# Where six-part modulation vectors are computed: parts moved from matmuls beside the linear attention to VectorE beside the MLPs

## The chip, the cores and the metric

The kernel runs on one core of a Trainium2 chip. Its time is the device time of one execution in microseconds (us), lower is better. The engines are named as in the profile: PE (TensorE's matmuls, PEld its weight loads), DVE (VectorE), ACT (ScalarE), POOL (GpSimd) and SP (the queue that issues most DMAs).

## The reference

Two layers process 512 latent tokens and 256 context tokens of width 1024 in float32. Each layer scales and shifts its normalised input with vectors that depend on a conditioning vector ("adaLN"). There are six parts of 1024 columns for each layer, and they are needed for the latent stream (from `c`) and, in layer 0 and for the first two parts of layer 1, for the context stream (from `c_ctx`):

```python
mod_l = jnp.split((jax.nn.silu(c) @ ada_w[layer] + ada_b[layer])[:, None, :], 6, axis=-1)
mod_c = jnp.split(jax.nn.silu(c_ctx) @ ada_w[layer] + ada_b[layer], 6, axis=-1)
ul = modulate(lat, g[0], mod_l[0], mod_l[1])            # mixer input
lat = lat + mod_l[2] * rmsnorm(yl @ w_out[layer], g[1])
lat = lat + mod_l[5] * rmsnorm(sq_relu_mlp(modulate(lat, g[2], mod_l[3], mod_l[4]), mlp_w1[layer], mlp_w2[layer]), g[3])
if ctx_out:                                             # layer 0 only: the same for cx with mod_c
    ...
```

So part 5 of layer 0 is first needed behind the second product of layer 0's MLP, parts 0 and 1 of layer 1 right behind that, parts 2 to 4 behind layer 1's mixer, and part 5 of layer 1 at the very end. Layer 0 mixes with gated linear attention beside grouped-query attention, layer 1 with an mLSTM beside retention. One part is a vector times a 1024 x 1024 matrix, 4 MB of weights.

## The kernel before

**Order of the work.** The program runs startup (parts 0 and 1 of layer 0, first projections), the linear attention stage ("GLA"), softmax attention, the output projection, the MLP of layer 0 over 768 tokens, the mixer of layer 1, its output projection, and the MLP of layer 1 over 512 tokens. The source order is written out by hand in strings (`PLAN`, line 133): each letter is one step of a generator. In "gla", `G` is a quarter of one of four head pairs of the linear attention, `q` a tile of the query projection, `a` one step of modulation, `l` a deferred piece of query preparation. In "mlp", `h` is a hidden tile (first product), `P` a piece of the second product, `s` one step of modulation from the side generator. Both strings of "mlp" are used for blocks 0 to 5 of eight; block 6 has a fixed string with nine `s`, and the last product calls the side generator at four of its token tiles ("side", line 139). The framework then orders the instructions of each engine by that source order and by its own cost estimates, so an engine's final order is near the source order, not equal to it.

**Matmuls.** A float32 product is made as three products of rounded halves (`mm3`, lines 488 to 490). The high half is a cast on ACT (`split`, L197), the low half a subtraction on DVE (L198). Weights pass through `raw`, a ring of three 128 x 1024 tiles that weights and modulation loads share; split weights go into rings of five. In the MLP the second product is made with seven instead of eight block products, for which POOL subtracts weight blocks (L638), DVE subtracts activations (L675) and adds up results (L744, first ones copied on ACT, L742).

**Modulation in the GLA stage** (`ada_steps`, L245): two parts at a time, eight steps; each step loads two 512 KB tiles (issue L257) and makes four column-tiled matmuls (L260, 32 of 128 columns each, both streams at once, each recorded as two instructions). `ada_finish` (L267) then fills two tiles on POOL (L271, L272), loads bias and gain, adds on DVE (L280) and stores. Three pairs of parts are made so: layer 0 parts 2 and 3, layer 0 parts 4 and 5, layer 1 parts 0 and 1.

**Modulation in layer 0's MLP** (`ada_part`, L293): layer 1 parts 2 to 5, latent stream only. A part has two column halves; each is summed over eight row blocks on DVE (first L310, then seven times L312, all 128 x 512), four loads of 512 KB (issue L303) to a half. A `yield` stands behind each issue, so one `s` treats the tile loaded by the `s` before and issues the next load. Then two matmuls with a matrix of ones (L315) sum over the partitions into a PSUM tile of tag "B", which the hidden tiles use too, and `ada_rows` (L319) fills two tiles on POOL (L324, L325), loads bias and gain (L329, L331), adds and scales on DVE (L332, L333) and stores (L335). The accumulators are a ring of two (`sp` in pool `p5`).

Of the kernel before, what the change touches and what calls it, by code (L numbers as in the profile page):

```python
# [8 lines left out]
F32 = mybir.dt.float32  # L9
# [3 lines left out]
ALU = mybir.AluOpType  # L13
# [109 lines left out]
def const_offsets():  # L123
# [8 lines left out]

PLAN = {
    "start": "tttttt",
    "gla": "GaGaGaqGaalGaaGalaqaaaGaGGlGlaaaqGaaaGaGlGlaqGGaaa",
    "att": "QQSSSSQSSSfSVSfSSSVSfSSSVfQSSSVSSVSSSVfQfVSSVVSfVSVQSSVSSVfVSVSSVSVSSVSVSVMSVSMVVSSVSSSVVSVMVVVVVVVM",
    "pre": 7,
    "l1": "tPPPtPPDtPPPPPPPLPzzPPPLzzFgUFLFwgULBgFwgwwwYUwwMBMMMBURBRRwR",
    "side": [1, 2, 3, 4],
    "mlp": ["sPhPPshPPhsPPhsP", "PhPPhPPhPPhP"],  # L140
    "ahead": (3, 3),
}

# [1 line left out]
class Kern:  # L145
# [144 lines left out]
                nc.sync.dma_start(out=cut(md[j]), in_=bt[r, :])  # L290
            self.mod[layer, part] = (md, 0)

    def ada_part(self, layer, part, pool):  # L293

        nc = self.nc
        W = self.a["ada_w"][layer]
        c0 = part * 1024
        md = self.T(self.dram, [1, 1024])
        acc = [self.T(pool, [128, 512], F32, tag="sp", bufs=2) for _ in range(2)]
        for x in range(2):  # L300
            for kk in range(4):
                raw = self.T(self.w1, [128, 1024], F32, tag="raw", bufs=3)
                nc.sync.dma_start(out=raw.rearrange("p (k n) -> p k n", k=2),  # L303
                                  in_=W[kk * 256:(kk + 1) * 256, c0 + x * 512:c0 + (x + 1) * 512].rearrange("(k p) n -> p k n", p=128))
                yield
                for k in range(2):
                    w = raw[:, k * 512:(k + 1) * 512]
                    c = self.sT[:, 2 * kk + k, 0:1]
                    if kk == 0 and k == 0:
                        nc.vector.tensor_scalar(out=acc[x], in0=w, scalar1=c, scalar2=None, op0=ALU.mult)  # L310
                    else:
                        nc.vector.scalar_tensor_tensor(out=acc[x], in0=w, scalar=c, in1=acc[x], op0=ALU.mult, op1=ALU.add)  # L312
        ps = self.pb()
        for x in range(2):
            nc.tensor.matmul(ps[32 * x:32 * x + 32, :], self.ones, acc[x], start=True, stop=True)  # L315
        self.ada_rows(layer, part, ps, [(0, 0), (512, 0)], md)
        self.mod[layer, part] = (md, 0)

    def ada_rows(self, layer, part, ps, rows, md):  # L319
# [837 lines left out]
    def layer0(self):  # L1157
        nc, a = self.nc, self.a
        uT = self.new_uT(self.r1, TOK)
        acc = self.startup(uT)  # L1160
# [3 lines left out]
        with self.pool("mx") as mx:  # L1164
# [11 lines left out]
            with self.pool("ga") as ga:  # L1176
                self.C0 = self.load_consts(ga, _L0_CONST)
                lr = self.T(ga, [128, 6, 32])

                def ev0(t, ps):  # L1180
                    nc.scalar.copy(ak[:, t * 128:(t + 1) * 128], ps[:, 0:128])
                    nc.scalar.copy(av[:, t * 128:(t + 1) * 128], ps[:, 128:256])
                    nc.vector.tensor_copy(lr[:, t], ps[:, 256:288])
                self.proj_tok(W, [(2080, 256), (1536, 32)], uT, range(NT), ev0, True)
                gv = self.big(self.r2)
                tok4 = lambda ap, t: ap[:, :, t * 128:(t + 1) * 128]
                self.proj_tok(W, [(512, 512)], uT, range(NT),
                              lambda t, ps: nc.scalar.copy(tok4(gv, t), ps.rearrange("p (r n) -> p r n", r=4)), True)
                kst = self.att_keys(ak, gb, tabs[1])

                late = []

                def later(n=1):
                    for x in late:
                        for _ in range(n):
                            next(x, None)

                def ev2(t, ps):
                    late.insert(0, self.att_query(t, ps, gb, tabs[0], qs_d[t * 128:(t + 1) * 128, :]))
                    later()  # L1200
                qsteps = self.proj_steps(W, [(1568, 512)], uT, range(NT), ev2)
                ada = (x for layer, parts in ((0, (2, 3)), (0, (4, 5)), (1, (0, 1))) for x in self.ada_steps(layer, parts, self.po()))
                gla = self.gla(ga, [gqk[:, p] for p in range(4)], [gv[:, p] for p in range(4)], lr,
                               lambda p: nc.sync.dma_start(out=on_d[p * 128:(p + 1) * 128, :], in_=gqk[:, p]))
                ops = {"G": lambda: next(gla), "q": lambda: next(qsteps), "a": lambda: next(ada, None), "l": later}
                for c in PLAN["gla"].replace(" ", ""):
                    ops[c]()
                later(2)
                for _ in ada:
                    pass  # L1210
# [42 lines left out]
        with self.pool("xw", bufs=3) as xw, self.pool("h0") as h0:  # L1253
            with self.pool("p3") as p3:
                self.out_proj(0, ws, lambda i, k: (yT[i] if k < 4 else yA[i])[:, k % 4], self.x_in,
                              lambda t: self.xs1[t * 128:(t + 1) * 128, :], uT2, p3, xw, range(NT), 0)
            with self.pool("p5") as p5, self.pool("ya") as yap:
                ytile = lambda dt=F32: self.T(yap, [128, 1024], dt, tag="y", bufs=6)
                ya, mods, cur, rvw = [], {}, [], []
                W1 = a["cd_w_in"][0]  # L1260
                self.rv_d = self.T(self.dram, [TOK, 512])

                def acc(t):
                    if t == len(ya):
                        ya.append(ytile())
                    return ya[t]

                def rv_weights(k):
                    if k == 1:
                        big = self.T(self.r1, [128, 3072], F32R, tag="big", bufs=4)  # L1270
                        cur[2:] = [big[:, i * 1024:(i + 1) * 1024] for i in range(3)]
                    into = {0: None, 1: cur[2:4], 2: [ytile(F32R), ytile(F32R)] if k == 2 else None, 3: [cur[4], ytile(F32R)] if k == 3 else None}[k]
                    rvw.extend(self.w_unit(W1, [(2048, 512)], k, into))

                def done(t, m, y, ss):
                    stream = "ctx" if t < 2 else "lat"
                    if not mods:
                        self.next_u = self.new_uT(self.r2, TOK)
                        mods["ctx"] = [self.bcast(xw, l, part, "ctx", "xh", 3) for l, part in ((0, 5), (1, 1), (1, 0))]
                        big = self.T(self.r1, [128, 3072], F32, tag="big", bufs=4)  # L1280
                        mods["lat"] = [self.bcast(None, l, part, "lat", None, tile=big[:, i * 1024:(i + 1) * 1024])
                                       for i, (l, part) in enumerate(((0, 5), (1, 1), (1, 0)))]
                    gg, gs, sh = mods[stream]
                    if m == 0:
                        cur[0:2] = [self.T(xw, [128, 1024], F32, tag=tag, bufs=3) for tag in ("xl", "xl" if t < 2 else "xh")]
                    xt, u = cur[0:2]
                    nc.vector.tensor_tensor(out=u[:, m * 512:(m + 1) * 512], in0=y, in1=gg[:, m * 512:(m + 1) * 512], op=ALU.mult)
                    if m == 0:
                        nc.sync.dma_start(out=xt, in_=self.xs1[t * 128:(t + 1) * 128, :])
                        return  # L1290
                    for k in {0: (0,), 1: (1,), 3: (2,), 4: (3,)}.get(t, ()):
                        rv_weights(k)
                    self.post_halves(ss, xt, u, self.xs2[t * 128:(t + 1) * 128, :])
                    self.prep(xt, gs, sh, u, self.next_u, t * 128)

                self.ones = self.T(h0, [128, 32])
                nc.vector.memset(self.ones, 1.0)

                def side():

                    for part in range(2, 6):
                        yield from self.ada_part(1, part, p5)
                ada = side()
                full = [(0, 512), (512, 768)]
                self.mlp(0, uT2, TOK, (self.r1, self.r1), h0, acc, xw, (full, full), done, ada)
                for _ in ada:
                    pass
                for _ in self.spill_tok(2048, self.next_u, range(NT), self.rv_d, False, True, rvw, p5):
                    pass
# [375 lines left out]
    def layer1(self):  # L1685
# [101 lines left out]
        with self.pool("xw1", bufs=3) as xw, self.pool("h1") as h1, self.pool("p7") as p7:  # L1787
# [9 lines left out]
            def done(i, m, y, ss):  # L1797
# [7 lines left out]
                (nc.gpsimd if i == 3 and m == 0 else nc.vector).tensor_tensor(out=yg[:, m * 512:(m + 1) * 512], in0=y, in1=mods[0][:, m * 512:(m + 1) * 512], op=ALU.mult)  # L1805
                if m:
                    self.post_halves(ss, xt, yg, self.out[0, i * 128:(i + 1) * 128, :])
            self.mlp(1, uT3, 512, (self.r2, self.r2), h1, acc, xw, ([(0, 256), (256, 512)], [(0, 512)]), done)

    def body(self):  # L1810
        tc, nc = self.tc, self.nc
# [39 lines left out]
```

## Time and profile before

| what | value |
|---|---|
| median of three runs | 1749.84 us (1747.56 to 1750.02) |
| the profiled execution | 1746.07 us |
| its span, first to last instruction | 1744.4 us |
| mean granted TensorE clock | 0.981 of 2.4 GHz |
| busy share of the span | PE 95%, PEld 75%, DVE 65%, ACT 45%, POOL 15% |
| moved by DMA | 193.74 MB read, 25.30 MB written, mean 127 GB/s |

A wait is written "engine line <- releaser line". Times in windows are from the span's start. Stages by their instructions: startup to about 120 us, GLA 120 to 280, attention and output projection to about 505, layer 0's MLP to about 985, layer 1's mixer and output projection to about 1420, layer 1's MLP to the end. A matmul's duration includes its passage through the pipeline, so matmuls in a row overlap; the busy time counts such overlap once.

### The profile page before, as it was taken

What the parts mean: (1) busy time and instruction counts of PE and PEld (TensorE: products, weight loads), DVE (VectorE), ACT (ScalarE), POOL (GpSimd) and SP (SyncE); (2) the same over time, 40 slices, a digit from 0 to 9 for tenths busy, and PEclk for the clock granted to TensorE, in tenths of its full rate; (3) what the DMA queues carried; (4) which work ended last, traced back from release to release, by engine and by line L of the source; (5) the groups of instructions that cost most, each with busy time, mean ns of one, the idle gap of its engine ahead of it and who ended that gap; (6) DMA issues with size and microseconds to landing.
All of it is one profiled execution on the core that took longest, in us unless ns stands there. A gap on an engine that the chain in (4) does not pass through costs nothing.

```text
span 1744.4 us, 25127 instructions
## 1 busy us (share of the span) xinstructions
PE 1660.3 (95%) x9795; PEld 1316.5 (75%) x9795; DVE 1131.3 (65%) x1678; ACT 791.5 (45%) x1392; POOL 264.3 (15%) x216
## 2 busy tenths in 40 slices
PE   7998999999999999999999999978998999999998
PEld 5775555755778888888888878757887788888876
DVE  5435456465678558657668693466786676777876
ACT  5335435464345434334333454635552355445443
POOL 0000020100002211121120000164011112223210
PEclk9999999999999999999999999988996999999999
DMA  9415666231654224224123552234545533333322
GB/s 289 129 52 178 202 205 223 72 91 37 205 169 128 90 61 155 74 83 157 62 90 118 176 192 64 84 104 130 161 132 164 181 98 108 110 108 99 107 86 84
DMA packets 174746, 220.67 MB, mean 127 GB/s; under 512 B 17450, under 2 KB 112742, under 8 KB 174628
## 3 DMA queue, kind: packets, MB, share of 16 engines
q1 hardware_dynamic: 169444, 201.24, 36.7%
q0 software_dynamic: 5184, 17.83, 3.0%
q8 instruction: 77, 1.26, 0.3%
q14 instruction: 41, 0.34, 0.1%
HBM read 193.74 MB, written 25.30 MB: 126 GB/s over the span
## 4 chain that ended last, share of the span: by engine, by line
PE 77%; DVE 9%; DMA 6%; ACT 4%; issue 3%; SPq 1%; POOL 0%; DVEq 0%; ACTq 0%; POOLq 0%
PE x L488 21%; PE x L489 21%; PE x L490 21%; DMA x<-in_ada_w_dram 2%; PE x L1116 2%; PE x L260 2%; DVE x L198 2%; PE x L1107 1%; PE x L1093 1%; DMA x<-x 1%; ACT x L197 1%; PE x L1542 1%; PE x L957 1%; PE x L435 1%; PE x L1681 1%
## 5 line engine op out<-in xcount | busy, mean ns | idle before, releaser
L488 PE MATMUL x<-x,x 128*128 128x512 f32 (+2 forms) x2042 | 763.3, 375 | 12.1 <-ACT x L197 3.4
L489 PE MATMUL x<-x,x 128*128 128x512 f32 (+2 forms) x2050 | 762.8, 373 | 7.1 <-DVE x L198 7.1
L490 PE MATMUL x<-x,x 128*128 128x512 f32 (+2 forms) x2050 | 761.1, 372 | 0.1
L198 DVE TENSOR_TENSOR x<-x,x 128x1024 fp32r<-128x1024 f32 (+4 forms) x373 | 395.5, 1079 | 216.5 <-ACT x L197 211.4
L197 ACT CAST x<-x 128x1024 fp32r<-128x1024 f32 (+4 forms) x373 | 332.7, 911 | 388.4 <-PE x L489 181.3
L488 PEld LDWEIGHTS x<-x,x 128*128 128x128 f32 x2042 | 387.4, 190 | 91.1 <-ACT x L197 9.0
L489 PEld LDWEIGHTS x<-x,x 128*128 128x128 f32 x2050 | 389.1, 190 | 75.7 <-DVE x L198 11.7
L490 PEld LDWEIGHTS x<-x,x 128*128 128x128 f32 x2050 | 388.9, 190 | 70.6 <-issue 6.3
L638 POOL TENSOR_TENSOR x<-x,x 128x1024 f32<-128x1024 f32 x56 | 145.5, 2599 | 546.3 <-DMA x<-in_mlp_w_dram 250.2
L744 DVE TENSOR_TENSOR x<-x,x 128x512 f32<-128x512 f32 x225 | 143.9, 680 | 12.3 <-PE x L490 11.2
L689 ACT ACTIVATE x<-x 128x512 f32<-128x512 f32 (+4 forms) x96 | 44.3, 477 | 91.2 <-PE x L490 91.2
L312 DVE SCALAR_TENSOR_TENSOR x<-x,x,x 128x512 f32<-128x512 f32 x56 | 53.1, 948 | 20.8 <-DMA x<-in_ada_w_dram 19.9
L260 PE MATMUL x<-x,x 128*32 128x512 f32 x192 | 45.6, 604 | 7.5 <-DMA x<-in_ada_w_dram 7.4
L690 ACT ACTIVATE x<-x 128x512 f32<-128x512 f32 (+4 forms) x96 | 48.0, 516 | 2.1
L1095 DVE TENSOR_REDUCE x<-x 128x1 f32<-128x768 f32 (+1 forms) x48 | 36.6, 775 | 18.9 <-PE x L1093 18.7
L1116 PE MATMUL x<-x,x 128*64 128x512 f32 x112 | 44.2, 618 | 1.0 <-ACT x L1110 0.7
L1096 ACT ACTIVATE x<-x,x 128x768 f32<-128x768 f32 (+1 forms) x48 | 36.3, 757 | 12.5 <-DVE x L1095 12.3
L1107 PEld LDWEIGHTS x<-x,x 128*128 128x128 f32 x224 | 24.5, 141 | 22.9 <-issue 21.1
L675 DVE TENSOR_TENSOR x<-x 128x768 f32<-128x768 f32 (+1 forms) x28 | 38.4, 1371 | 0.0
L1093 PE MATMUL x<-x,x 128*128 128x256 f32 (+1 forms) x160 | 36.7, 347 | 1.3 <-ACT x L1096 1.3
L799 DVE TENSOR_REDUCE x<-x 128x8 f32<-128x512 f32 (+1 forms) x19 | 14.3, 753 | 35.5 <-ACT x L797 35.4
L797 ACT ACTIVATE x<-x 128x512 f32<-128x512 f32 (+1 forms) x19 | 12.8, 673 | 47.6 <-PE x L957 25.8
(316 smaller groups left out, 1517.8 us busy)
## 6 DMA issues: line engine op xcount, KB each, us to landing
x<-in_mlp_w_dram SPq DMA_DIRECT2D x128, 512.0 KB
x<-in_ada_w_dram SPq DMA_DIRECT2D x96, 512.0 KB
x<-x SPq DMA_DIRECT2D x42, 512.0 KB
x<-x SPq DMA_DIRECT2D x50, 256.0 KB
x<-in_cd_w_in_dram SPq DMA_DIRECT2D x24, 512.0 KB
x<-x POOLq DMA_DIRECT2D x36, 256.0 KB, 3.1
x<-in_ab_w_in_dram SPq DMA_DIRECT2D x16, 512.0 KB
x<-x SPq DMA_DIRECT2D x20, 384.0 KB
```

What stands on the lines that cost most here:

```text
L197: self.nc.scalar.copy(hi, src)
L198: self.nc.vector.tensor_tensor(out=lo, in0=src, in1=hi.bitcast(F32), op=ALU.subtract)
L260: nc.tensor.matmul(ps[32 * g:32 * g + 32, :n], self.sT[:, k, :], rs[g], start=k == 0, stop=k == 7)
L312: nc.vector.scalar_tensor_tensor(out=acc[x], in0=w, scalar=c, in1=acc[x], op0=ALU.mult, op1=ALU.add)
L488: mm(out, st[0], mv[0], start=start, stop=False, skip_group_check=partial)
L489: mm(out, st[0], mv[1], start=False, stop=False, skip_group_check=partial)
L490: mm(out, st[1], mv[0], start=False, stop=stop, skip_group_check=partial)
L638: sub = lambda out, x, y: nc.gpsimd.tensor_tensor(out=out, in0=x, in1=y, op=ALU.subtract)
L690: nc.scalar.activation(out=hh[:, f, c0:c1], in_=h[:, c0:c1], func=AF.Square)
L744: nc.vector.tensor_tensor(out=dst, in0=dst, in1=acc[j], op=ALU.add)
L1093: mm(pS[:, s0:s1], qs[:, h * 128:(h + 1) * 128], kst[kv][i][:, s0:s1], start=i == 0, stop=i == 1)
L1116: mm(po[64 * kv:64 * kv + 64, :], av[:, kt * 128 + kv * 64:kt * 128 + kv * 64 + 64], PT[kv], start=kt == 0, stop=kt == nk - 1)
```

## The change

- The GLA stage makes layer 0 parts 2 and 3 as before and part 4 alone (eight steps with one load each and four matmuls of 256 columns). Layer 0 part 5 and layer 1 parts 0 and 1 leave it. Eight `a` are taken out of the "gla" string (24 to 16); `G`, `q` and `l` stay in number and order.
- `ada_part` learns two streams: with `ns` = 2 it keeps two accumulators and does each DVE step twice, once with each stream's column of the conditioning; then each column half ends with its own pair of ones-matmuls and its own `ada_rows`. With `ns` = 1 (layer 1 parts 2 to 5) the two halves are finished together as before.
- The side generator of layer 0's MLP makes, in this order, layer 0 part 5, layer 1 parts 0 and 1 (two streams each), then layer 1 parts 2, 3, 4 (one stream). The block string has six `s` instead of four.
- Layer 1's MLP gets a side generator with layer 1 part 5, and two `s` in its block string. Its accumulators and the ones come from the ring of seven `t4` tiles.

```diff
@@ PLAN @@
-    "gla": "GaGaGaqGaalGaaGalaqaaaGaGGlGlaaaqGaaaGaGlGlaqGGaaa",
+    "gla": "GaGGaqGalGaaGlaqaaGaGGlGlaaqGaaGGlGlaqGGaa",
-    "mlp": ["sPhPPshPPhsPPhsP", "PhPPhPPhPPhP"],
+    "mlp": ["sPhsPPshPPhssPPhsP", "PhPPshPPhPPhsP"],
@@ ada_part @@
-        acc = [self.T(pool, [128, 512], F32, tag="sp", bufs=2) for _ in range(2)]
+        ns = 1 if layer == 1 and part > 1 else 2
+        held = []
         for x in range(2):
+            acc = [new() for _ in range(ns)]
+            held += [(j, x, acc[j]) for j in range(ns)]
             for kk in range(4):
...
                 for k in range(2):
                     w = raw[:, k * 512:(k + 1) * 512]
-                    c = self.sT[:, 2 * kk + k, 0:1]
-                    if kk == 0 and k == 0:
-                        nc.vector.tensor_scalar(out=acc[x], in0=w, scalar1=c, scalar2=None, op0=ALU.mult)
-                    else:
-                        nc.vector.scalar_tensor_tensor(out=acc[x], in0=w, scalar=c, in1=acc[x], op0=ALU.mult, op1=ALU.add)
-        ps = self.pb()
-        for x in range(2):
-            nc.tensor.matmul(ps[32 * x:32 * x + 32, :], self.ones, acc[x], start=True, stop=True)
-        self.ada_rows(layer, part, ps, [(0, 0), (512, 0)], md)
+                    for j in range(ns):
+                        c = self.sT[:, 2 * kk + k, j:j + 1]
+                        if kk == 0 and k == 0:
+                            nc.vector.tensor_scalar(out=acc[j], in0=w, scalar1=c, scalar2=None, op0=ALU.mult)
+                        else:
+                            nc.vector.scalar_tensor_tensor(out=acc[j], in0=w, scalar=c, in1=acc[j], op0=ALU.mult, op1=ALU.add)
+            if len(held) == 2:
+                ps = self.pb()
+                for i, (_, _, r) in enumerate(held):
+                    nc.tensor.matmul(ps[32 * i:32 * i + 32, :], self.ones, r, start=True, stop=True)
+                self.ada_rows(layer, part, ps, [(y * 512, j) for j, y, _ in held], md)
+                held = []
@@ layer0 @@
-                ada = (x for layer, parts in ((0, (2, 3)), (0, (4, 5)), (1, (0, 1))) for x in self.ada_steps(layer, parts, self.po()))
+                ada = (x for layer, parts in ((0, (2, 3)), (0, (4,))) for x in self.ada_steps(layer, parts, self.po()))
...
-                    for part in range(2, 6):
-                        yield from self.ada_part(1, part, p5)
+                    for layer, part in ((0, 5), (1, 0), (1, 1), (1, 2), (1, 3), (1, 4)):
+                        yield from self.ada_part(layer, part, lambda: self.T(p5, [128, 512], F32, tag="sp", bufs=2))
@@ layer1 @@
-            self.mlp(1, uT3, 512, ..., done)
+            t4 = lambda: self.T(p7, [128, 1024], F32, tag="t4", bufs=7)
+            self.ones = t4()[:, :32]
+            nc.vector.memset(self.ones, 1.0)
+            self.mlp(1, uT3, 512, ..., done, self.ada_part(1, 5, lambda: t4()[:, :512]))
```

## Rows read from the trace of the kernel before

**Rows 1.** The page, part 1: busy time and share of the span by engine.

```profile
PE 1660.3 (95%) x9795; PEld 1316.5 (75%) x9795; DVE 1131.3 (65%) x1678; ACT 791.5 (45%) x1392; POOL 264.3 (15%) x216
```

**Rows 2.** Busy time by stretch of the span, all engines; the header names the columns.

```profile
core 0: us, PE busy (x) PEld busy (x) DVE busy (x) ACT busy (x) POOL busy (x), PEclk, DMA share, GB/s
120.00:280.00 160.00, 142.44 (x1814) 83.14 (x1812) 74.75 (x125) 70.10 (x129) 16.55 (x20) 0.99 0.58 192
...
520.00:760.00 240.00, 240.00 (x1261) 206.53 (x1260) 162.97 (x182) 105.06 (x158) 49.10 (x22) 1.00 0.33 102
...
980.00:1040.00 60.00, 57.87 (x276) 47.01 (x276) 52.20 (x113) 32.43 (x78) 1.51 (x3) 1.00 0.52 175
1420.00:1660.00 240.00, 240.00 (x1088) 199.94 (x1088) 181.49 (x205) 124.52 (x180) 60.51 (x23) 1.00 0.34 104
```

**Rows 3.** The chain that ended last, 120 to 280 us, shares by line.

```profile
by line: DMA x<-in_ada_w_dram 22.3%; PE x L260 19.5%; PE x L957 7.5%; PE x L488 5.0%; PE x L490 5.0%; PE x L489 4.5%; PE x L858 4.4%; PE x L954 4.1%; DMA x<-in_ab_w_in_dram 3.5%; issue 2.8%; PE x L879 1.9%; ACT x L913 1.8%; ACT x L865 1.5%;
```

**Rows 4.** PE's busy time in L260 alone, 120 to 290 us.

```profile
120.00:290.00 170.00, 45.60 (x192) 6.57 (x192) 0.99 0.58 191
```

**Rows 5.** PE's busy time in L385 alone (256 columns, 32-column tiles), startup.

```profile
0.00:60.00 60.00, 8.44 (x128) 3.34 (x128) 0.97 0.93 265
```

**Rows 6.** PE's waits, 120 to 280 us: total us, times, longest.

```profile
PE x L260 <- DMA x<-in_ada_w_dram: 7.4, 7, 2.2
PE x L858 <- DVE x L852: 2.7, 2, 1.9
```

**Rows 7.** PE in order of time, one stretch of a head pair: start, us, what.

```profile
205.58 0.49 PE L858 MATMUL x<-x,x 128*128 128x384 f32 x1
206.00 1.05 PE L260 MATMUL x<-x,x 128*32 128x512 f32 x4
206.98 0.91 PE L858 MATMUL x<-x,x 128*128 128x384 f32 x2
```

**Rows 8.** ACT's first gate step of each head pair: ns min/median/max, first and last start.

```profile
L849 ACT ACTIVATE x<-x x4: 811/812/814, 133.6 to 233.5; 128x768 f32<-128x768 f32 x4
```

**Rows 9.** Groups of PE, DVE and POOL, 500 to 980 us.

```profile
L315 PE MATMUL x<-x,x 128*32 128x512 f32 x16 | 4.2, 604 | 0.0
L312 DVE SCALAR_TENSOR_TENSOR x<-x,x,x 128x512 f32<-128x512 f32 x56 | 53.1, 948 | 20.8 <-DMA x<-in_ada_w_dram 19.9
L310 DVE TENSOR_SCALAR x<-x,x 128x512 f32<-128x512 f32 x8 | 3.9, 483 | 21.5 <-PE x L315 17.7 <-DMA x<-in_ada_w_dram 3.9
L638 POOL TENSOR_TENSOR x<-x,x 128x1024 f32<-128x1024 f32 x28 | 72.6, 2591 | 322.2 <-DVE x L198 132.4 <-DMA x<-in_mlp_w_dram 117.3 <-issue 71.9
```

**Rows 10.** L312 as one line: ns min/median/max, first and last start.

```profile
L312 DVE SCALAR_TENSOR_TENSOR x<-x,x,x x56: 736/752/2908, 521.5 to 949.8; 128x512 f32<-128x512 f32 x56
```

**Rows 11.** DVE's busy time in L312 alone, 520 to 760 us.

```profile
520.00:760.00 240.00, 32.20 (x28) 1.00 0.33 102
```

**Rows 12.** DVE groups by form, 525 to 920 us: the end of a part.

```profile
L333 DVE SCALAR_TENSOR_TENSOR x<-x 64x512 f32<-64x512 f32 x3 | 2.0, 676 | 0.0
L332 DVE TENSOR_TENSOR x<-x,x 64x512 f32<-64x512 f32 x3 | 2.0, 672 | 0.0
```

**Rows 13.** DVE's waits, 520 to 760 us: total us, times, longest.

```profile
DVE x L198 <- ACT x L197: 52.9, 21, 6.5
DVE x L312 <- DMA x<-in_ada_w_dram: 10.8, 6, 3.9
DVE x L310 <- PE x L315: 6.0, 1, 6.0
```

**Rows 14.** SP's waits, 525 to 920 us: weight loads behind modulation.

```profile
SPq L594 <- DVE x L312: 46.7, 16, 8.0
```

**Rows 15.** DVE and POOL in order of time at the MLP's start.

```profile
521.50 9.95 DVE L312 SCALAR_TENSOR_TENSOR x<-x,x,x 128x512 f32<-128x512 f32 x5
...
521.96 8.16 POOL L638 TENSOR_TENSOR x<-x,x 128x1024 f32<-128x1024 f32 x3 [30.56 <-DMA x<-in_mlp_w_dram]
```

**Rows 16.** Busy time by stretch, columns as in rows 2: DVE almost full.

```profile
520.00:540.00 20.00, 20.00 (x124) 18.02 (x123) 19.67 (x15) 8.13 (x11) 11.27 (x4) 1.00 0.49 151
920.00:940.00 20.00, 18.80 (x84) 15.26 (x83) 19.38 (x26) 6.73 (x8) 0.00 (x0) 1.00 0.22 72
```

More of the change, by code (lines that the diff above doesn't have):

```diff
@@ L291, in ada_finish, with ada_part @@
             self.mod[layer, part] = (md, 0)
-    def ada_part(self, layer, part, pool):
+    def ada_part(self, layer, part, new):
         nc = self.nc
@@ L297, in ada_part @@
         c0 = part * 1024
-        md = self.T(self.dram, [1, 1024])
-        acc = [self.T(pool, [128, 512], F32, tag="sp", bufs=2) for _ in range(2)]
+        ns = 1 if layer == 1 and part > 1 else 2
+        md = self.T(self.dram, [2, 1024])
+        held = []
         for x in range(2):
+            acc = [new() for _ in range(ns)]
+            held += [(j, x, acc[j]) for j in range(ns)]
             for kk in range(4):
@@ L1807, in done @@
                     self.post_halves(ss, xt, yg, self.out[0, i * 128:(i + 1) * 128, :])
-            self.mlp(1, uT3, 512, (self.r2, self.r2), h1, acc, xw, ([(0, 256), (256, 512)], [(0, 512)]), done)
+            t4 = lambda: self.T(p7, [128, 1024], F32, tag="t4", bufs=7)
+            self.ones = t4()[:, :32]
+            nc.vector.memset(self.ones, 1.0)
+            self.mlp(1, uT3, 512, (self.r2, self.r2), h1, acc, xw, ([(0, 256), (256, 512)], [(0, 512)]), done, self.ada_part(1, 5, lambda: t4()[:, :512]))
     def body(self):
```

## The prediction

> **What bounds the kernel now.** I read the page first: PE is busy 95% of the span, no other engine over 75%, DVE 65% [rows 1]. So what the change is worth is PE time removed, less PE time added and less the waits that PE gets. Then the stretches. From 120 to 280 us (the GLA stage) PE is busy 142.44 of 160 us; DVE and ACT are under half [rows 2]. In layer 0's MLP, 520 to 760 us, PE is busy 240.00 of 240 us with DVE at 162.97 [rows 2]: PE alone is the bound there, and DVE has 77 us to spare. The same holds in layer 1's MLP: PE 240.00, DVE 181.49 of 240 [rows 2]. Third, the chain of waits in the GLA stage: modulation loads are 22.3% of it and the modulation matmuls L260 19.5%, more than any step of the linear attention itself [rows 3]. In the trace they also stand inside its steps: four L260 instructions cut into the cumulative sums L858 and delay what ACT waits for by 0.98 us [rows 7]. A head pair comes every (233.5 - 133.6) / 3 = 33.3 us [rows 8].
>
> **PE time removed in the GLA stage.** L260 costs 45.60 us for three pairs of parts, 15.2 us a pair [rows 4]. Two pairs go: -30.4. Part 4 alone comes back: 8 steps of 8 instructions with 256 columns, like startup's L385, 8.44 us for 128: 64 cost 4.2 us [rows 5]. Net -26.2 us of PE.
>
> **Waits there.** PE is idle 160 - 142.44 = 17.6 us; 7.4 of it waits for modulation loads [rows 2, 6]. Loads fall from 48 of 512 KB to 24, and eight of the 16 steps left need one load instead of two. I take 5 of the 7.4 as gone. One of three finishing rounds (two POOL fills, the small loads and stores on SP) goes too; as neither queue is the bound, I cost that at nothing. Against this, modulation matmuls covered the latencies of the linear attention. PE's work without L260 is 142.4 - 45.6 = 97 us, with what is left of L260 116; the four head pairs, one behind another, need 4 x 33.3 = 133 us now, of which some 9 of a pair's 33 us are L260 (about nine groups of 0.98 us as in rows 7). Without half of those a pair takes about 29 us, 115 in all. So PE and the chain would be nearly equally long, which costs idle time at both. Bounds: nothing gets exposed (the gain is 26.2 + 7.4 = 33.6), or the chain holds the stage after about half of the removed PE time (13). I take 8 us exposed: -26.2 - 5 + 8 = **-23 us**. The 8 stands nearest to the 10.2 us that PE already waits here for other things than modulation loads.
>
> **PE time added.** A pair of ones-matmuls, recorded as four instructions, costs 4.2 / 4 = 1.05 us [rows 9]. Before there are four such ends in layer 0's MLP. After there are nine (two for each of three two-stream parts, one for each of three others), and one in layer 1's MLP: 6 x 1.05 = **+6.3 us**, all on the bounding engine.
>
> **DVE in layer 0's MLP.** The two-stream parts take 24 loads x 4 operations. With two calls ahead and six `s` a block, all lie in the first four blocks, about 520 to 760 us. One operation takes (7 x 752 + 483) / 8 = 0.72 us undisturbed [rows 9, 10]. Now 28 L312 and some 4 L310 run there [rows 11]; after, 96. That is 64 x 0.72 = 46 us more, and 4 more ends at 0.67 + 0.68 us, 5.4 us [rows 12]. DVE rises from 163 to 214 of some 244 us. Disturbance comes on top: L312's mean is 948 ns against the median 752 [rows 9, 10], so 56 more L312 at 0.196 each give 11 us: 225 of 244, 92%. The six single-stream halves behind it and 13 us for part 5 in layer 1's MLP (16 x 0.72 + 1.35; DVE 181 to 194 of 240) I cost at nothing beyond the ones-matmuls: DVE's idle time covers them. Without that cover it would be their DVE time, 13 us in layer 1's MLP.
>
> What does a nearly full DVE cost PE? Two rows bound it. From 520 to 540 us DVE is busy 19.67 of 20 us and PE loses nothing; from 920 to 940 it is busy 19.38 and PE loses 1.2 [rows 16]. Over twelve such stretches that is 0 to 14 us. DVE also stood 6.0 us behind L315 within 520 to 760 us [rows 13], while PE was busy 240.00 [rows 2]: the split weights are far enough ahead. The first end is likelier at 92% than at 98%. But the tight spot is the MLP's start, where 16 operations instead of eight stand ahead of the first activation splits, in a stretch without DVE slack. I take **+6 us**, mostly there. An `s` also holds a `raw` slot twice as long, and behind it on SP wait the next hidden tile's weights (46.7 us in 16 waits already [rows 14]); that is the way by which a late DVE reaches PE, and is in the 6. Five more ends add ten POOL fills of half a microsecond and some 25 small DMAs to queues that are mostly idle: nothing, as long as they are not ahead of a late weight load.
>
> **The disturbance, and a rule on it.** Five L312 took 9.95 us while POOL ran three L638 in 8.16 us [rows 15]: 2 us each instead of 0.75. The Trainium skill, SBUF — State Buffer, "Who interferes with whom", says that a VectorE instruction with two SBUF inputs and a GpSimd instruction that reads SBUF share a port by an exclusive lock, so the later fully waits. The trace agrees: an L312 of up to 2908 ns is a median one plus most of an L638 [rows 9, 10]. By the rule alone, if each L638 of these blocks (22) held one L312 for 2.16 us, the disturbance would be 47 us and not 17 (11 added to some 6 now in 28 operations), and DVE would be over-full; that is the last rival below.
>
> **The end of layer 0's MLP.** 47 side calls come before the last product, 49 are needed. So two loads' operations (4 x 0.72) and an end (1.35) fall into 960 to 1040 us, where DVE is at 52.20 of 60 us and PE idles 2.1 [rows 2]. Bounds 0 and 4.2; **+2 us**.
>
> **Sum**: -23 + 6.3 + 6 + 2 = -8.7 us. The profiled execution took 1746.07 us (1744.4 of span and 1.7 around it), so it would take 1737.4. The median of the runs is 3.8 us above the profiled one, which gives 1741.1, rounded to **1741**.
>
> **The rivals.**
> - *The DVE work is free.* The stalls of 6 and 2 us don't come: 1749.8 - 23 + 6.3 = 1733 us. For it: PE 240.00 of 240 beside a 6 us DVE wait. Against it: 920 to 940 us.
> - *The linear attention's own chain takes over* in the GLA stage. The gain there is 13 - 1, say 12 us, and all losses stay: -12 + 6.3 + 6 + 2 = +2, 1752 us, no difference or slower. For it: ACT and DVE each wait on the other and on PE there and are under half busy [rows 2]. Against it: the chain's largest shares are modulation [rows 3].
> - *VectorE becomes the bound in blocks 0 to 3.* DVE needs 225 us; if half of its 52.9 us behind ACT and all of its 14.7 behind loads stay as they are (10.8 for L312 and 3.9 for L310 [rows 9, 13]), it needs 266, and 244 are there: 22 us late instead of 6. -23 + 6.3 + 22 + 2 = +7, **1757 us**, slower. It decides from the point at which work and waits that remain exceed 244 us; at 19 us left over, half of today's 77, it does not. For it: the port held by POOL, in-order waits. Against it: DVE's waits behind ACT are mostly those of an engine that is ahead, and vanish when it falls back.
>
> **Chances.** Forecast 0.42, free DVE 0.20, GLA chain 0.18, DVE bound 0.20. What can be told from no change is 0.2%, 3.5 us. Faster: 0.40 of the forecast, 0.20, and 0.03 of the third: 0.63. Same: 0.02, 0.12 and 0.03 of the last: 0.17. Slower: 0.03 and 0.17: 0.20. The likeliest case alone spans 1735 to 1746 us. The range of 1729 to 1758 takes in the rivals' times; it leaves out the free case with nothing exposed (below 1729, some 0.05) and an over-full DVE beyond 22 us (some 0.10).
>
> **What would show it.** In the changed profile L260 must have 128 instructions and about 19 us, the ones-matmuls 40 instructions and 10.5 us, L312's counterpart 140. The GLA stage, from its first L260 to the last head pair's end, must be 18 to 28 us shorter, with PE's wait for modulation loads near 2 us. In layer 0's MLP, PE's waits must name DVE for about 6 us in all, around the first blocks. I am wrong if PE idles over 15 us there, if L312's mean rises far over 948 ns, or if the head pairs still come every 31 us or more.

## The result and the profile after

The changed kernel takes 1732.39 us (1731.73 to 1734.44) beside 1748.7 us (1745.82 to 1750.02) before: ratio 0.9911 [0.9894, 0.9928], 16 us less. A second session gave 0.9901 [0.9880, 0.9923]. The forecast was 9 us less, 1741 us. The profiled executions stand at 1746.07 and 1732.92 us, 13.2 us apart; the other 3 us are within the scatter of single executions, told behind the table.

I cut both spans at events that both traces have: the last score matmul of the attention, the first transpose of the preparation for layer 0's MLP, the first result of its last product, the last transpose of layer 1's preparation.

| stage, us | before | after | change |
|---|---|---|---|
| start to the key transposes | 124.9 | 125.5 | +0.6 |
| GLA and attention, to the last score | 287.8 | 260.3 | **-27.5** |
| to the MLP's preparation | 48.9 | 49.1 | +0.2 |
| layer 0's MLP, to its last product | 527.1 | 537.3 | **+10.2** |
| its end, layer 1's mixer and projection | 426.2 | 427.3 | +1.1 |
| layer 1's MLP | 329.5 | 331.7 | +2.2 |

The fifth stage is not touched by the change but for two late side calls; in the fourteen profiles of this study it took from 415.4 to 429.6 us, while layer 0's MLP in the changed kernel took 537.3 and 537.4 us in two sessions. So totals of single executions scatter by more than the effects, and stages are the finer measure. They are not equally fine. Layer 0's MLP took 526.2 to 527.1 us in the four profiles that leave it as before. The GLA stage took 260.3 to 265.6 us in the ten profiles with the changed steps, and 293.0 beside 287.8 us in a second profile with the steps of before. So the -27.5 is one pair; the means of these profiles differ by 28, and a single pair is good to some 5 us.

The page after, part 1, answers to [rows 1]:

```profile
PE 1649.5 (95%) x9755; PEld 1320.8 (76%) x9755; DVE 1224.0 (71%) x1783; ACT 790.6 (46%) x1392; POOL 276.9 (16%) x226
```

The two changed stages of the kernel before, busy time by stretch (PE, PEld, DVE, ACT, POOL, then granted clock, DMA share, GB/s):

```profile
124.90:412.70 287.80, 268.05 (x2431) 164.52 (x2430) 159.93 (x255) 146.97 (x288) 26.49 (x30) 0.99 0.47 155
...
461.60:988.70 527.10, 523.16 (x2681) 444.55 (x2682) 362.30 (x458) 214.70 (x329) 78.08 (x39) 1.00 0.37 116
```

The same two of the changed kernel:

```profile
125.50:385.80 260.30, 241.97 (x2366) 163.34 (x2365) 157.37 (x251) 145.42 (x288) 25.03 (x28) 0.97 0.38 123
...
434.90:972.20 537.30, 531.35 (x2698) 447.21 (x2699) 436.05 (x547) 214.44 (x329) 90.32 (x49) 0.99 0.40 128
```

In the first stage PE's busy time falls by 26.1 us and its idle time from 19.75 to 18.33: nothing was given back. In the second PE is busy 8.2 us longer and idle 2.0 us longer, with DVE up by 74 us.

PE's modulation matmuls in the GLA stage of the changed kernel (busy, instructions), its waits there (total us, times, longest), and the first gate step of a head pair, answering to [rows 4, 6, 8]:

```profile
120.00:290.00 170.00, 19.35 (x128) 4.03 (x128) 0.96 0.43 145
```

```profile
PE x L942 <- ACT x L920: 3.6, 3, 1.6
PE x L961 <- DVE x L951: 2.8, 2, 1.5
PE x L260 <- DMA x<-in_ada_w_dram: 2.8, 3, 1.8
```

```profile
L856 ACT ACTIVATE x<-x x4: 792/808/815, 134.1 to 221.8; 128x768 f32<-128x768 f32 x4
```

The matmuls shrank by 26.25 us, the wait for loads by 4.6, and a head pair comes every 29.2 us instead of 33.3. The waits on the attention's own chain (L942, L961) grew, but are small. In the kernel before they were:

```profile
PE x L935 <- ACT x L913: 1.5, 1, 1.5
PE x L954 <- DVE x L944: 0.5, 1, 0.5
```

In layer 0's MLP DVE and POOL start like this, in order of time (answers to [rows 15]):

```profile
495.44 13.14 DVE L317 SCALAR_TENSOR_TENSOR x<-x,x,x 128x512 f32<-128x512 f32 x10
...
495.32 8.08 POOL L645 TENSOR_TENSOR x<-x,x 128x1024 f32<-128x1024 f32 x3 [30.61 <-DMA x<-in_mlp_w_dram]
```

and PE has two stops of 2 us that the kernel before lacks or has shorter (1.2 us at the second place [rows 16]), each next to a lower clock (columns as above):

```profile
515.00:520.00 5.00, 2.99 (x19) 2.38 (x18) 5.00 (x7) 2.33 (x4) 0.00 (x0) 1.00 0.54 160
520.00:525.00 5.00, 5.00 (x17) 3.92 (x16) 4.97 (x6) 2.40 (x5) 0.00 (x0) 0.66 0.75 234
930.00:935.00 5.00, 3.05 (x10) 2.11 (x10) 4.41 (x5) 1.04 (x1) 0.00 (x0) 0.82 0.41 122
935.00:940.00 5.00, 5.00 (x22) 4.08 (x21) 2.06 (x4) 1.05 (x1) 0.00 (x0) 0.84 0.93 291
```

Ten L317 took 13.14 us where ten undisturbed ones take 7.5. The first activation splits then came late, PE stood 2.0 us at 515 us, and in the 5 us after it the granted clock was 0.66, partly the lower level of 1.2 GHz: 5 x 0.34 = 1.7 us more. The second stop comes with as much, 5 x 0.18 + 5 x 0.16 = 1.7. So of the 8.2 us that PE is busy longer, 4.2 are four more ends of ones-matmuls, 3.4 the clock, and 0.6 are not placed. The interval from the preparation to the first added result grew from 96.4 to 100.6 us. The second stop has an ACT wait for hidden weights ahead of it, which share the `raw` ring with the modulation loads.

### The profile page after: what moved, and what is told of

Same layout as the page of the kernel before. It is cut to its first block, busy times and chain, and to the rows that moved or that the text cites. A ratio compares the mean times of both kernels' runs of the same rounds, so it can differ in the third digit from the quotient of the medians.

```text
span 1731.2 us, 25197 instructions
## 1 busy us (share of the span) xinstructions
PE 1649.5 (95%) x9755; PEld 1320.8 (76%) x9755; DVE 1224.0 (71%) x1783; ACT 790.6 (46%) x1392; POOL 276.9 (16%) x226
## 4 chain that ended last, share of the span: by engine, by line
PE 76%; DVE 11%; DMA 5%; ACT 4%; issue 3%; SPq 1%; POOL 0%; DVEq 0%; ACTq 0%; POOLq 0%
PE x L495 20%; PE x L496 20%; PE x L497 20%; PE x L1123 2%; DVE x L198 2%; PE x L1100 1%; PE x L1114 1%; DMA x<-x 1%; DMA x<-in_mlp_w_dram 1%; ACT x L197 1%; DMA x<-in_ada_w_dram 1%; PE x L1548 1%; DVE x L317 1%; PE x L1687 1%; PE x L865 1%
## 5 line engine op out<-in xcount | busy, mean ns | idle before, releaser
L198 DVE TENSOR_TENSOR x<-x,x 128x1024 fp32r<-128x1024 f32 (+4 forms) x373 | 405.4, 1107 | 153.4 <-ACT x L197 148.6
L495 PEld LDWEIGHTS x<-x,x 128*128 128x128 f32 x2042 | 389.1, 191 | 99.0 <-ACT x L197 13.2
L645 POOL TENSOR_TENSOR x<-x,x 128x1024 f32<-128x1024 f32 x56 | 153.7, 2744 | 506.1 <-DMA x<-in_mlp_w_dram 244.9
L317 DVE SCALAR_TENSOR_TENSOR x<-x,x,x 128x512 f32<-128x512 f32 x140 | 124.9, 926 | 17.6 <-DMA x<-in_ada_w_dram 16.9
L1102 DVE TENSOR_REDUCE x<-x 128x1 f32<-128x768 f32 (+1 forms) x48 | 36.9, 774 | 10.6 <-PE x L1100 10.3
L434 ACT ACTIVATE x<-x 128x1024 f32<-128x1024 f32 x16 | 17.0, 1061 | 39.7 <-DVE x L452 28.4
L682 DVE TENSOR_TENSOR x<-x 128x768 f32<-128x768 f32 (+1 forms) x28 | 33.9, 1210 | 0.0
L1114 PE MATMUL x<-x,x 128*128 128x128 f32 x224 | 33.4, 280 | 0.0
```

Of the source, the lines that this page charges most:

```text
L198: self.nc.vector.tensor_tensor(out=lo, in0=src, in1=hi.bitcast(F32), op=ALU.subtract)
L317: nc.vector.scalar_tensor_tensor(out=acc[j], in0=w, scalar=c, in1=acc[j], op0=ALU.mult, op1=ALU.add)
L495: mm(out, st[0], mv[0], start=start, stop=False, skip_group_check=partial)
L645: sub = lambda out, x, y: nc.gpsimd.tensor_tensor(out=out, in0=x, in1=y, op=ALU.subtract)
L1114: nc.tensor.transpose(pt[:, g * 128:(g + 1) * 128], P[kv][:, g, kt * 128:(kt + 1) * 128], self.C["ident"])
```

## The experiments

All were timed in five rounds beside the kernel before; "stage" is a stage of the table above. The edits of the first three are against the kernel before, those of the others against the changed kernel.

**Only the GLA side of the change.**

```diff
-    "gla": "GaGaGaqGaalGaaGalaqaaaGaGGlGlaaaqGaaaGaGlGlaqGGaaa",
+    "gla": "GaGGaqGalGaaGlaqaaGaGGlGlaaqGaaGGlGlaqGGaa",
...
-                ada = (x for layer, parts in ((0, (2, 3)), (0, (4, 5)), (1, (0, 1))) for x in self.ada_steps(layer, parts, self.po()))
+                ada = (x for layer, parts in ((0, (2, 3)), (0, (4,))) for x in self.ada_steps(layer, parts, self.po()))
...
+                for x, y in (((0, 5), (0, 2)), ((1, 0), (0, 3)), ((1, 1), (0, 4))):
+                    self.mod[x] = self.mod[y]
```

> The kernel before with only the part of the change that lies in the GLA stage: 16 steps instead of 24, three parts not computed (other parts' vectors stand in for them), the MLPs as before. My prediction's term for this was -23 us. Both theories read from the two traces say more: in the changed kernel the last attention score comes 26.9 us earlier, so I expect -27 us (-24 to -30). If it is -23 or less, the rest of the gain came from somewhere else, behind the stage.

Measured: 1719.98 us, ratio 0.9854 [0.9827, 0.9881], -25.5 us; GLA and attention 260.8 us, -27.0. By stage the gain is 27 us and lies there; layer 0's MLP takes 526.2 us as before. The total's interval, about 5 us to either side, would by itself not exclude the forecast's -23.

**The loads stay, the matmuls go.** Part 4 is made alone with part 5's tile loaded beside it, and eight steps follow that load layer 1's parts 0 and 1; nothing reads these tiles.

```diff
+            for h in range(nw, nw + extra):
+                raw = self.T(self.w1, [128, 1024], F32, tag="raw", bufs=3)
+                nc.sync.dma_start(out=raw, in_=W[k * 128:(k + 1) * 128, c0 + h * 1024:c0 + (h + 1) * 1024])
...
+                def steps3():
+                    yield from self.ada_steps(0, (2, 3), self.po())
+                    yield from self.ada_steps(0, (4,), self.po(), 1)
+                    yield from loads()
```

**The matmuls stay, the loads go.** `nl` loads to a step: two, then one, then none; an activation tile (`still`) is multiplied where none is loaded.

```diff
-            for h in range(nw):
+            for h in range(min(nw, nl)):
...
+            while len(rs) < 4:
+                rs.append(rs[-2] if rs else still)
+                if len(rs) == 1:
+                    rs.append(still)
```

> As the kernel with fewer GLA steps, but all 48 loads of 512 KB stay in the stage; only the matmuls of the three parts are left out (these parts are not computed). Theory PE time: the gain is the matmuls' busy time, 26 us, so -21 to -27 us remain. Theory loads: the gain comes from the waits behind the loads and from the shared ring, so the time falls by 12 us at most.

> The kernel before with all matmuls and steps of the GLA stage but without the loads of the three parts (their matmuls read a tile that is already there, so the three parts are not computed). Theory PE time: -3 to -8 us, PE's wait for modulation loads falls from 7.4 us to under 4 and nothing else changes. Theory loads: -15 us or more.

Measured: without the matmuls 1728.39 us, 0.9895 [0.9868, 0.9922], -18.3 us, stage 269.3 us (-18.5). Without the loads 1737.82 us, 0.9960 [0.9940, 0.9980], -7.0 us, stage 281.1 us (-6.7). The first missed its bracket of 21 to 27 by 3 us: unread loads still cost the stage, PE idles 25.57 us in it instead of 19.75. The second did not leave PE's time alone, as its expectation had it. Its modulation matmuls (L260, here L264), all 192 instructions, took 31.91 us instead of 45.60 [rows 4], and from the second pair of parts on a step's four matmuls mostly stand together:

```profile
120.00:290.00 170.00, 31.91 (x192) 5.59 (x192) 0.97 0.42 134
...
201.25 1.07 PE L264 MATMUL x<-x,x 128*32 128x512 f32 x8
```

Eight recorded instructions took 1.07 us here. In the kernel before a step comes mostly in two halves of four, each 1.05 us [rows 7]; its two tiles are loaded one by one, which is the likely reason. So in the stage PE is busy 10.6 us less than before and idle 3.9 us more, and the 6.7 us are no measure of the waits for loads. That the two runs add up to some 25 us shows nothing. What the loads cost is better read between the kernel without the matmuls and the first experiment: 269.3 and 260.8 us with the same 128 instructions, 8.5 us, of which 6.9 are PE's idle time. By that pair some two thirds of the gain are PE time and one third the loads. The second theory, at most 12 us without the matmuls and 15 or more without the loads, falls. Each kernel also has another order by the planner, so a few us could be its doing.

**Only the MLP side of the change**, the GLA stage as before.

```diff
-    "gla": "GaGGaqGalGaaGlaqaaGaGGlGlaaqGaaGGlGlaqGGaa",
+    "gla": "GaGaGaqGaalGaaGalaqaaaGaGGlGlaaaqGaaaGaGlGlaqGGaaa",
...
-                ada = (x for layer, parts in ((0, (2, 3)), (0, (4,))) for x in self.ada_steps(layer, parts, self.po()))
+                ada = (x for layer, parts in ((0, (2, 3)), (0, (4, 5)), (1, (0, 1))) for x in self.ada_steps(layer, parts, self.po()))
```

> The changed kernel's MLPs with the GLA stage of before, which computes the three parts a second time. My prediction's terms for the MLPs were +6.3 (ones-matmuls) +6 (late DVE) +2 (end of the MLP) = +14.3 us. If the two parts of the change add up, this and the kernel with fewer GLA steps must sum to the measured -16: I expect +11 us (+8 to +14). Rival: the MLPs cost under 6 us, and the GLA stage gave what was forecast.

Measured: 1756.91 us, ratio 1.0066 [1.0042, 1.0090], +11.5 us; layer 0's MLP 535.2 us, +8.1. With the first experiment's -25.5 that makes -14.0; the whole change is -15.6 [-18.5, -12.6] by its ratio. The halves add up within the intervals. But in the profile 5.2 us of the loss lie in the GLA stage, whose steps are those of before:

```profile
124.90:417.90 293.00, 273.06 (x2431) 166.49 (x2430) 159.81 (x255) 147.27 (x288) 26.45 (x30) 0.97 0.48 152
```

PE is busy 5.0 us longer there at a granted clock of 0.97 instead of 0.99, and idle as long as before (19.94 us). That is no cost of the change.

**One stream instead of two on DVE.**

```diff
-        ns = 1 if layer == 1 and part > 1 else 2
+        ns = 1
```

> The changed kernel with one stream in all side parts: 48 loads as before it, but 24 loads' DVE operations halved (48 fewer of 0.72 us) and three ends fewer; the context stream takes the latent stream's vectors for three parts, so these are not computed. Theory stalls: PE's two stops in layer 0's MLP (2.0 us each at 515 and 931 us, each followed by some 1.7 us of lost clock) come from a full DVE; the first goes and the time falls by 3 x 1.05 + 3.7 = 7 us (5 to 10). Rival, DVE work is free: -3.2 us, the ends alone.

Measured: 0.9884 [0.9865, 0.9903]; layer 0's MLP 527.5 us, 9.8 less than in the changed kernel and 0.4 more than before. The stop at 515 us is gone, the one at 931 us is not (PE waits 1.9 us for ACT). The DVE work of the second stream and its three ends cost that stage 10 us: 3.2 us are the ends, 2.7 PE's idle time, and 3.4 the clock, which stays at 1.00 here. By the totals it is only 3 to 5 us less than the changed kernel, under the bracket.

**POOL fills instead of subtracts.**

```diff
-            sub = lambda out, x, y: nc.gpsimd.tensor_tensor(out=out, in0=x, in1=y, op=ALU.subtract)
+            def sub(out, x, y):
+                for _ in range(2):
+                    nc.gpsimd.memset(out, 0.01)
```

> The changed kernel with POOL's weight differences replaced by two fills each, which only write (the second product of the MLPs is then not the reference's). Theory lock: a DVE operation with two inputs waits for a POOL operation that reads, so L317's mean falls from 926 ns to about 750 and the first DVE block of eleven operations from 13.1 us to about 8; the stop at 515 us goes with it and the time falls by 2 to 6 us. Rival: the slow operations have another cause (loads landing, PE), the mean stays over 880 ns and the time within 1.5 us.

Measured: 0.9863 [0.9844, 0.9883]; layer 0's MLP 531.7 us, 5.6 less. The total gained more, but its unchanged fifth stage happened to take only 415.4 us. L317 of this kernel (ns min/median/max), then the changed kernel's:

```profile
L317 DVE SCALAR_TENSOR_TENSOR x<-x,x,x x140: 728/747/753, 498.7 to 1506.3; 128x512 f32<-128x512 f32 x140
```

```profile
L317 DVE SCALAR_TENSOR_TENSOR x<-x,x,x x140: 734/746/2936, 495.4 to 1524.3; 128x512 f32<-128x512 f32 x140
```

Not one of 140 operations is slow when POOL only writes, though 40 of them ran beside a fill; in the changed kernel twelve took over 1 us, and all twelve overlap one of POOL's subtractions. The slow ones are thus waits for POOL's reading operations, and the stop at 515 us went with them. The stop at 931 us stayed (1.9 us), but without the lower clock beside it, so 1.7 of the 5.6 us are a fall of the clock that is not tied to POOL.

**Side calls later.** The late start has no side call ahead of block 0 and two more in block 6:

```diff
         for _ in hidden2(0):
-            next(side, None)
+            if n <= 512:
+                next(side, None)
...
-            for c in PLAN["mlp"][0 if n > 512 else 1] if b < 6 else "PsPsPsPsPsPPhshshshs":
+            for c in PLAN["mlp"][0 if n > 512 else 1] if b < 6 else ("PsPsPsPsPsPPhsshsshshs" if n > 512 else "PsPsPsPsPsPPhshshshs"):
```

The late-and-early kernel has the first of these edits, and in place of the second one:

```diff
+            order = PLAN["mlp"][0 if n > 512 else 1] if b < 6 else "PPPPPPPhshshshs" if n > 512 else "PsPsPsPsPsPPhshshshs"
+            if n > 512 and b in (4, 5):
+                order = "ssPhssPPshPPhssPPhssP"
```

> The changed kernel without the two side calls ahead of block 0 of layer 0's MLP, two more in block 6: all is computed. Theory start: the stop at 515 us comes from the operations of the first loads standing ahead of the first activation splits; it goes with its lost clock and 2 to 4.5 us are gained. Rival: the planner puts as much work there anyway, or the two calls cost as much in block 6: within 1.5 us.

> As the late start, and the side calls of block 6 (nine) become four, behind its hidden tiles; blocks 4 and 5 get nine instead of six: all is computed. Theory ring: the stop at 931 us comes from modulation loads that hold the ring of raw tiles ahead of the hidden tiles' weights (ACT waits 11.9 and 5.2 us for such weights); it goes too and 5 to 8 us are gained against the changed kernel, which makes it the fastest version. Rival: only the first stop goes, or the fuller blocks 4 and 5 stop PE in its place: 0 to 4 us.

Measured: 0.9958 [0.9942, 0.9973] and 0.9959 [0.9943, 0.9975]; layer 0's MLP 538.1 and 543.2 us: longer than in the changed kernel, not shorter. Both theories missed. By their ratios both kernels lost 8 to 10 us in total on the changed kernel; of the late start's this stage explains 0.8, and the rest is not explained. The weights now came earlier, so POOL's three subtractions ran ahead of the end of the preparation. The late start's DVE and POOL in order of time:

```profile
492.09 8.07 POOL L645 TENSOR_TENSOR x<-x,x 128x1024 f32<-128x1024 f32 x3 [24.73 <-DMA x<-in_mlp_w_dram]
...
495.72 2.04 DVE L209 SCALAR_TENSOR_TENSOR x<-x,x 128x1 f32<-128x1 f32 x1
497.80 0.15 DVE L213 TENSOR_SCALAR x<-x 128x1 f32<-128x1 f32 x1
497.98 2.19 DVE L214 TENSOR_TENSOR x<-x,x 128x1 f32<-128x1 f32 x1
```

and its PE waits there:

```profile
PE x L442 <- DVE x L439: 8.6, 3, 7.4
```

Two operations on a single column with two inputs took 2 us each, while the one with one input took 0.15. PE's transposes waited 7.4 us behind them. What looked like a matter of how much modulation work stands at the start is one of what POOL does beside it.

**Block 0's weight differences on DVE; all of layer 0's on DVE; block 6 alone.** Beside the changed kernel once more. The edit for block 0 follows; "all" is the same without `and b == 0`, and "block 6 alone" is the `order` of the late-and-early kernel with the start left as it is.

```diff
-            sub = lambda out, x, y: nc.gpsimd.tensor_tensor(out=out, in0=x, in1=y, op=ALU.subtract)
+            sub = lambda out, x, y: (nc.vector if n > 512 and b == 0 else nc.gpsimd).tensor_tensor(out=out, in0=x, in1=y, op=ALU.subtract)
```

> The changed kernel unaltered, timed once more beside three variants of it, since the experiments before were timed in other sessions. Expected: a ratio to before within 0.989 to 0.993, layer 0's MLP (first transpose of its preparation to the first step of its end) 536 to 539 us long.

> The changed kernel with the four weight differences of block 0 of layer 0's MLP made on DVE instead of POOL; all is computed. Theory lock: what delays the first splits is not the 16 modulation operations (12 us undisturbed) but their blocking by POOL, about 5 us in the first eleven; DVE pays 4 x 1.2 us, of which one or two stand ahead of the first splits, and the stop at 515 us and its lost clock go: -2 to -4.5 us in layer 0's MLP. Rival, amount of DVE work: DVE has 5 us more to do there, the stop stays or grows: 0 to +5 us.

> The changed kernel with all weight differences of layer 0's MLP on DVE; all is computed. The kernel with POOL fills was 5.6 us shorter in this stage, and it left the subtractions out. DVE gets 28 x 1.2 = 34 us more and loses what POOL blocked, at most 28 x 2.2 us. Theory lock: -1 to -5 us in the stage. Rival, amount of DVE work: 0 to +10 us, DVE over 90% busy over the whole stage.

> The changed kernel with its start as it is, but four side calls instead of nine in block 6 and nine instead of six in blocks 4 and 5; all is computed. Theory ring: the stop at 931 us goes with its lost clock and nothing comes in its place: -2 to -4 us in layer 0's MLP. Rival: in the late-and-early kernel PE lost 0.4 to 0.6 us in each of three stretches behind 740 us instead, so it is the fuller blocks that cost: -1 to +3 us.

Measured, total and layer 0's MLP: changed kernel again 0.9901 [0.9880, 0.9923], 537.4 us; block 0 on DVE 0.9891 [0.9868, 0.9914], 531.6 us; all on DVE 0.9897 [0.9875, 0.9919], 531.2 us; block 6 alone 0.9923 [0.9899, 0.9947], 534.8 us. The kernel with block 0 on DVE, whole stage and the stretch in which the first stop lay:

```profile
436.50:968.10 531.60, 527.77 (x2697) 444.98 (x2698) 433.83 (x550) 214.03 (x328) 76.65 (x45) 1.00 0.41 130
```

```profile
515.00:540.00 25.00, 25.00 (x133) 20.71 (x132) 15.94 (x19) 16.08 (x27) 0.00 (x0) 1.00 0.34 103
```

Its preparation-to-first-result interval is 96.5 us, as before the change (96.4): four subtractions moved onto the engine that seemed too full, and the whole cost of block 0 went. The planner also put them between the modulation operations, so order has a share in it. The stage gave 5.8 us, more than the 2 to 4.5 expected: 2.2 us are PE's idle time and 3.4 the clock, half of that at the second stop, which is still there. With all subtractions on DVE nothing more is gained. Whether the move would help the kernel before as much was not tried. In total the gain on the changed kernel is inside the intervals, so a faster version is not shown, a shorter stage is. Block 6 alone lost its stop at 931 us, but a new one came at 900 to 920 us:

```profile
900.00:920.00 20.00, 16.68 (x73) 13.16 (x72) 20.00 (x27) 7.25 (x10) 0.00 (x0) 1.00 0.21 79
```

DVE is full there, 20.00 of 20: the fuller blocks took the stop over, so the ring's share stays open. The stage's 2.6 us are not a gain in waits, since PE idles 6.43 us in it instead of 6.05. They are the clock, which stood at 1.00 also beside this kernel's first stop of 2.0 us:

```profile
510.00:520.00 10.00, 7.99 (x47) 6.79 (x46) 10.00 (x9) 4.33 (x9) 2.00 (x1) 1.00 0.45 138
520.00:525.00 5.00, 5.00 (x24) 4.14 (x23) 4.97 (x7) 4.22 (x6) 0.00 (x0) 1.00 0.46 147
```

## Why the prediction was wrong

The direction held, and so did the main mechanism, PE time removed in one stage and added in another; the size did not, mainly by one term.

- **PE time removed, -26.2.** L260 went from 45.60 to 19.35 us, -26.25. Right.
- **Waits for loads, -5.** 7.4 to 2.8 us, -4.6. Right by PE's named waits; between the two kernels with the same 128 instructions the loads cost 8.5 us, so they also delay what no wait puts down to them.
- **Exposed latency, +8: the step that failed.** I argued that PE's 116 us and a chain of 115 us, being equally long, would cost idle time at both. PE's idle time without the load waits went from 19.75 - 7.4 = 12.4 to 18.33 - 2.8 = 15.5 us: +3, not +8. Against the second profile with the steps of before (19.94 - 10.2 = 9.7 us) it is +6, still under 8. The head pairs did come every 29 us, as forecast, so the removed matmuls had been in their way as well as filling PE's gaps. The 8 came from the 10.2 us of other waits, which were no measure of what would open. The stage gave 27 us, not 23. That the term was too large is shown, its size only to a few us: PE's busy time fell by 26.1 us against the first profile and by 31.1 against the second, at the same granted clock of 0.97. Where the loads stayed, the other idle time did rise by 8 (25.57 - 5.1 = 20.5 us), so the loads had a part in it; why the rest stayed covered is not shown.
- **Ones-matmuls, +6.3.** 40 instructions, 1.05 us an end; four of the five new ends in layer 0's MLP lie ahead of its last product and make 4.2 of the stage's 10.2 us. Right.
- **A late DVE, +6.** The stage's other 6.0 us. The size is right by luck. The place was right (the start of block 0 gave 4.2), but PE's waits were to name DVE for about 6 us, and only 2.0 us are idle time; 3.4 are the clock, which the prediction did not have. And the cause was a collision with POOL more than an amount of work: without it the stage stands 4.5 us over the kernel before (531.6 and 527.1), little more than the four ends. DVE was busy 206.83 us of the 240 from 495 to 735 us, under the 214 to 225 that I counted; its waits behind ACT there fell from 52.9 us to 19.9, as the last rival's counterargument had it.
- **The end of layer 0's MLP, +2.** PE idled 2.0 us of 60 in the matching stretch, 2.1 before [rows 2]: nothing. DVE had room.
- **Layer 1's MLP**, +1.05 forecast, +2.2 in this pair of profiles; in ten profiles with the change it took 330.8 to 332.6 us, in four without it 329.5 to 330.7. The rest isn't explained.

So -27.5 in the place of -23, and 0 for +2, are 6.5 of the 7.6 us between forecast and measured change; the remaining 1 us is less than the untouched stage scatters. The time came out at the rival "DVE work is free" (1733 us), but that isn't what happened: the MLP paid its 10 us, and the GLA stage gave more. "The chain takes over" and "VectorE becomes the bound" are refuted by the stages, -27.5 and +10.2 for -12 and over +26.

The rule cited ahead, of the port that VectorE and GpSimd hold in turn (the Trainium skill, SBUF — State Buffer, "Who interferes with whom"), is borne out beyond what I used: the same section says that a GpSimd instruction that only writes does not block such a VectorE instruction, and with fills L317's longest was 753 ns instead of 2936. What I had worked out by it, 47 us if every subtraction held one L317, did not come: from 495 to 735 us 76 L317 took 65.1 us, some 8 more than at their median.

Two slips in the working left the forecast as it is. The 22 POOL instructions of [rows 2] include four fills, so the 47 us should be 18 x 2.16 = 39. And 19 us are a quarter of DVE's 77, not half; with half of them left over, the rival "VectorE becomes the bound" would have decided.

## What to carry to other kernels

Work that filled an engine between the steps of a chain stood in the chain's way here as well: when such work goes, count its removal in full, and charge exposure only where the trace shows the chain waiting with the engine idle. Before putting work on an engine with idle time, look at what it shares a port with at that place; the amount was harmless here, three POOL operations beside it were not. When a variant takes out one half of a cause, look whether it left the other half alone: the kernel without the loads also lost 13.7 us of matmul time. And when single executions scatter by more than the effect, cut the span at events that both traces have, and learn from repeated profiles how far each stage scatters.

## What was not expected of the hardware

- A PE stop of 2.0 us in a stretch at full clock was followed by 5 us at a granted clock of 0.66, so it cost 3.7 us; but with block 0 on DVE a stop of 2.0 us between 920 and 940 us left the clock at 1.00, and so did the block-6 kernel's stop of 2.0 us between 510 and 520 us. What decides it is not shown. The GLA and attention stage stood at 0.99 in the kernel before and at 0.95 to 0.97 in the thirteen other profiles, also in the one with the steps of before and the same idle time: that fall is not the change's doing.
- Four column-tiled matmuls (eight recorded instructions) took 1.07 us together; two of them alone (four instructions) took 1.05.
- One-column DVE operations with two inputs took 2.04 and 2.19 us beside POOL; the same two lines took 0.22 and 0.16 us elsewhere in that preparation. Such waits hit the shortest operations of a chain hardest.
- With fills in place of POOL's subtractions the one-input operation L315 took up to 1255 ns beside a fill, and 486 at the median: a POOL that only writes does not leave every DVE operation alone.
